# A fused two-layer block: which expert pairs of the first mixture return their rows by way of DRAM

## The chip, the core and the metric

The kernel runs on one core of a Trainium2 chip. The metric is device time in microseconds for one execution of the whole program, from inputs in DRAM to the output in DRAM; lower is better. Engines are named as in the profile: PE (TensorE) does matmuls, DVE (VectorE), ACT (ScalarE) and POOL (GpSimd) do elementwise work, SP and POOL issue DMAs. The core has 16 DMA engines that all queues share.

## The reference

Two transformer-like blocks follow each other. Each has a mixer (attention beside a recurrence), a residual addition and a mixture of experts; the second block ends in a norm that gives the output. All is in float32 with 512 tokens of width 1024. What the change touches is the first mixture: 32 experts in four groups, each token goes to the best group and there to its two best experts.

```python
def hier_moe(x2d, w_grp, b_grp, w_exp, b_exp, w_gate, w_up, w_down):
    ...
    combine = jnp.sum(jax.nn.one_hot(global_idx, N_EXPERTS, dtype=jnp.float32) * weights[..., None], axis=1)
    y = jnp.zeros_like(x2d)
    for e in range(N_EXPERTS):
        h = jax.nn.silu(x2d @ w_gate[e]) * (x2d @ w_up[e])
        y = y + combine[:, e:e + 1] * (h @ w_down[e])
    return y
...
        y = hier_moe(xn, ...)
        h = h + y.reshape(B, S, D)
```

Each expert has gate and up weights of 1024 x 256 and down weights of 256 x 1024. `combine` has two nonzero entries in a row, so a kernel need compute each expert for its own tokens alone.

## The kernel before

**Units.** The first mixture, `moe1`, works in 16 units of two experts each. An expert has 64 slots for tokens in a round, so a unit has 128 rows: expert 2u in rows 0 to 63, expert 2u+1 in rows 64 to 127. A loop behind the first round (`For_i` in `moe_rounds`, L1589) runs further rounds for experts with more than 64 tokens; here its count is zero, but every engine still loads the count (L1588), branches past the body and meets the others at a barrier, which also waits for all DMAs in flight.

**A unit's steps.** POOL gathers the unit's token rows from DRAM (`gather`, L1596, into `xg`). PE transposes them (`gathered`, L1609), multiplies by gate and up weights (L1711, `mm`), ACT and DVE make the hidden row (L1714, L1715), PE transposes it (`turned`, L1765), and in the next turn of the loop PE multiplies it by the down weights (`product`, L1655, `ua`). In the trace a float32 matmul shows as two records.

**Two ways back.** What a unit yields has to be added to the right rows of `h`, the residual stream, which stays in SBUF as four tiles of 128 tokens.

- One-hot: `down` scales the product and splits it into a high and a low half (ACT L1785, DVE L1786, tiles `oh`), and `scatter` (L1793) lets PE multiply a one-hot matrix `SC` (made by DVE, L1790) by both halves. It does so for two units at once, one half of the columns (`d`) at a time: four matmuls (L1806, L1807) for each tile of `h`, 16 for a half, summed in one PSUM bank, then one DVE add into `h` (L1800). Two banks, `ch` and `pq`, alternate.
- By DRAM: `by_dram` scales the product (ACT L1664, tile `ot`) and POOL scatters the rows to a DRAM buffer `yd` (L1665). Once the last such unit has been written, eight indirect DMAs (L1730), two for each tile of `h`, gather every token's rows from `yd` and accumulate them into `h` in SBUF. An entry of the row table out of bounds is left out.

`FROM[1]` and `BYDRAM[1]` (L28, L29) say in experts which go by DRAM: `far` (L1681) is units 4 to 13. Units 0 to 3 go by one-hot products in pairs, in the turns 3 to 6. Unit 14 and unit 15 are handled last: the down product of unit 14 is made at the start of turn 15 (`y14`), that of unit 15 behind the loop (`end`), and their one-hot products form the final pair.

**Weights.** SP loads the experts' weights, 1 MB a DMA and 96 in all (`ring_load`, L1540), into a ring of tiles `ew` in the order in which PE uses them: gate and up of a unit, then the down weights of the unit before; for unit 15 the down weights of unit 14 come first. Up to eight are in flight.

**Order.** The tile scheduler places instructions on the engines from the program's order and its own priorities; each engine runs its own list in order. In the turns from unit 9 on, the down product of a `by_dram` unit stands split on PE: two matmuls early, six later, with transposes between.

Of the kernel before, what the change touches and what calls it, by code (L numbers as in the profile page):

```python
# [24 lines left out]
SIGMOID = "sigmoid_and_others"  # L25
SILU = "silu_and_others"

FROM = {1: 8, 2: 0}  # L28
BYDRAM = {1: 20, 2: 14}  # L29
CAP = {1: 64, 2: 96}  # L30
ZROW = {k: BYDRAM[k] * CAP[k] for k in CAP}
# [38 lines left out]
def host_consts(inp):  # L70
    pc = {part: np.zeros((128, n), np.float32) for part, n in LAY.n.items()}

    def put(name, a):
        part, o, w = LAY.at[name]
        pc[part][:, o:o + w] = a

    def cols(v):
        v = np.asarray(v).reshape(-1, 128)
        return v.T
# [22 lines left out]
    for k, e in (1, np.arange(32)), (2, np.arange(16)):  # L102
        put("row%d" % k, one * np.where((e >= FROM[k]) & (e < FROM[k] + BYDRAM[k]), CAP[k] * (e - FROM[k]), 1e5))
    put("out1", i[:, None] + 128 * np.arange(16) - CAP[1] * FROM[1])
    put("g_f2", cols(inp["ffn_norm_2"]))
# [77 lines left out]
class Kern:  # L183
# [1459 lines left out]
    def moe1(self):  # L1643
# [6 lines left out]
        def product(hT, w, d):  # L1650

            p = self.ps("dn")
            for k in range(2):
                for a in range(2):
                    nc.tensor.matmul(p[hs(a)], hT[:, k, hs(a)], w[a][:, k * 1024 + d * 512:k * 1024 + d * 512 + 512],  # L1655
                                     start=k == 0, stop=k == 1)
            return p
# [10 lines left out]

        def down(hT, w, wt, SC, at=None):

            hl = []
            for d in range(2):
                y = at[:, d] if at is not None else yp.tile([128, 2, 512], R32, tag="o%d" % d, name="oh%d" % d, bufs=2 + d)
                hl.append([y[:, 0], y[:, 1]])
                self.rows_hl(*hl[d], product(hT, w, d), wt)
            return SC, hl

        def body(num, wts, idx, first):

            ys, prev = [], None  # L1680
            far = range(FROM[1] // 2, (FROM[1] + BYDRAM[1]) // 2) if first else ()  # L1681
            for u in range(2):
                ins = self.gather(xgs[u], mo, idx, u)
            if first:
                with tc.issue_after(ins.ins):
                    mo.ahead += [self.moe_load(mo, nc.gpsimd) for _ in range(mo.late)]
            nx = self.gathered(gp, xgs[0], False)

            def down_args(u, hT, num, wts):
                return hT, [self.moe_next(mo) for _ in range(2)], wts[:, u:u + 1], onehot(u, yp.tile([128, T], R32, name="SC", bufs=3))  # L1690

            onehot = lambda u, SC: self.onehot(SC, mo, num, u)
            for u in range(mo.U):
                xT, _ = nx
                if u + 2 < mo.U:
                    self.gather(xgs[u % 2], mo, idx, u + 2)
                last = u == mo.U - 1
                if last and first:
                    SC = self.place(mo, 2, R32)
                    y14 = down(prev[1], [self.moe_next(mo) for _ in range(2)], wts[:, u - 1:u], onehot(u - 1, SC[:, 0:T]),  # L1700
                               self.place(mo, 2, R32).rearrange("p (d i c) -> p d i c", d=2, i=2))
                elif last:
                    self.scatter(ys[12:14], 0)
                    ys.append(down(*down_args(*prev, num, wts)))
                w = [self.moe_next(mo) for _ in range(4)]
                p = self.ps("gu")
                for m in range(2):
                    d = p[:, m * 256:m * 256 + 256]
                    for k in range(KD):
                        for a in range(2):  # L1710
                            nc.tensor.matmul(d[hs(a)], xT[:, k, hs(a)], w[2 * m + a][:, k * 256:k * 256 + 256],  # L1711
                                             start=k == 0, stop=k == KD - 1)
                hh = gp.tile([128, 256], F32, name="hh", bufs=1)
                nc.scalar.activation(hh, p[:, 0:256], AF.Silu)  # L1714
                nc.vector.tensor_tensor(hh, hh, p[:, 256:512], OP.mult)  # L1715
                if last:
                    break
                nx = self.gathered(gp, xgs[(u + 1) % 2], False)

                e = (u - 3) // 2 * 2  # L1720
                if e >= 0 and (not first or e < far[0]):
                    self.scatter(ys[e:e + 2], (u + 1) % 2)
                if prev and prev[0] in far:
                    by_dram(*prev)
                elif prev:
                    ys.append(down(*down_args(*prev, num, wts)))
                if far and u == far[-1] + 1:
                    for c in range(2):
                        for n in range(NT):
                            nc.gpsimd.indirect_dma_start(  # L1730
                                out=self.h[:, n], out_offset=None, in_=self.yd,
                                in_offset=bass.IndirectOffsetOnAxis(ap=mo.row[:, n, c:c + 1], axis=0),
                                bounds_check=ZROW[1] - 1, oob_is_err=False, compute_op=OP.add)
                hT = gp.tile([128, 2, 128], F32, name="hT", bufs=1)
                turned(hh, hT)
                prev = u, hT
            if not first:
                self.scatter(ys[12:15], 1)
                self.scatter(ys[14:15], 0)
                hT = gp.tile([128, 2, 128], F32, name="hT", bufs=1)  # L1740
                turned(hh, hT)
                return first, None, *down_args(mo.U - 1, hT, num, wts)

            keep, gs = self.place(mo, 2), self.place(mo, 3)
            hT, wt = keep[:, 0:256].rearrange("p (k t) -> p k t", k=2), keep[:, 256:257]
            nc.vector.tensor_copy(wt, wts[:, mo.U - 1:mo.U])
            SC = onehot(mo.U - 1, SC[:, T:2 * T])
            turned(hh, hT)
            w = [self.moe_next(mo) for _ in range(2)]

            raw, hl = keep[:, D:2 * D], self.place(mo, 3, R32).rearrange("p (i k c) -> p i k c", i=2, k=KD)
            nc.sync.dma_start(raw, self.ap["win2"][4])
            raw = raw.rearrange("p (k c) -> p k c", k=KD)
            nc.scalar.activation(hl[:, 0], raw, AF.Copy)
            nc.gpsimd.tensor_tensor(hl[:, 1], raw, hl[:, 0], OP.subtract)
            self.early.append((hl[:, 0], hl[:, 1]))
            self.rows = gs[:, 0:D], gs[:, D:]
            for t, nm in zip(self.rows, ("fin_g", "attn_g")):
                nc.sync.dma_start(t, self.ap[nm].to_broadcast([128, D]))
            return first, y14, hT, w, wt, SC  # L1760
# [279 lines left out]
```

## Time and profile before

| | |
|---|---|
| median of three runs | 1422.45 us (1418.68 to 1423.33) |
| profiled execution | 1419.69 us, its span 1417.9 us |
| PE busy | 1289.0 us, 91% of the span |
| DVE, ACT, POOL busy | 841.6, 701.6, 410.2 us |
| HBM read, written | 270.70 MB, 22.29 MB |
| mean granted PE clock | 0.965 of full speed |
| chain that ended last | PE 68%, DVE 13%, DMA 11%, ACT 3%, issue 2% |

The span is the time from the first to the last instruction of one profiled execution; all times of day below count from its start. The first mixture runs from about 462 to 722 us. A share of DMA is the mean busy share of the 16 engines. "[1.63 <-DMA x]" behind a row says that the engine had been idle for 1.63 us and what ended it.

### The profile page before, as it was taken

To read this page: it belongs to the slowest core of one execution; us is meant where nothing else is said; L and a number is where in the kernel's file an instruction comes from. 1 tells how busy PE (TensorE), PEld (TensorE's weight loads), DVE (VectorE), ACT (ScalarE), POOL (GpSimd) and SP (SyncE) were. 2 spreads that over 40 slices of the span, in tenths; PEclk is the share of its full clock that TensorE was granted. 3 is DMA by queue.
4 is the path that set the end of the run, shared out by engine and by line. 5 is a ranking of instruction groups with operands and counts; after the bars stand their busy time and mean duration, and the time that the engine had idled before them with its cause. 6 is when DMAs were issued, how large, how long until landed. Compare 5 with 4: busy or idle time off the path is not lost.

```text
span 1417.9 us, 20482 instructions
## 1 busy us (share of the span) xinstructions
PE 1289.0 (91%) x7792; PEld 927.7 (65%) x7792; DVE 841.6 (59%) x1432; ACT 701.6 (49%) x1217; POOL 410.2 (29%) x329
## 2 busy tenths in 40 slices
PE   7999999999897999999379999999996999999993
PEld 5777766767696555554156776777894666666662
DVE  4679866566656131000075656657637799998895
ACT  6433433334634221211064555555545788888883
POOL 1000224241104101110366102011124555555445
PEclk9999999999998899999789999999997999999996
DMA  5232440000484999999832121202386999889943
GB/s 189 75 89 75 107 109 2 1 1 2 188 330 170 386 419 419 418 418 422 223 101 75 30 76 45 86 24 100 105 334 209 321 360 382 320 332 391 385 166 125
DMA packets 54452, 283.93 MB, mean 200 GB/s; under 512 B 8849, under 2 KB 9745, under 8 KB 28738
## 3 DMA queue, kind: packets, MB, share of 16 engines
q1 hardware_dynamic: 43634, 254.75, 47.9%
q0 software_dynamic: 9840, 26.39, 5.8%
q8 instruction: 66, 1.08, 0.3%
q10 hardware_dynamic: 864, 1.31, 0.3%
q14 instruction: 48, 0.39, 0.1%
HBM read 270.70 MB, written 22.29 MB: 207 GB/s over the span
## 4 chain that ended last, share of the span: by engine, by line
PE 68%; DVE 13%; DMA 11%; ACT 3%; issue 2%; POOL 1%; SPq 0%; DVEq 0%; POOLq 0%; ACTq 0%
PE mm L322 12%; PE ua L1903 4%; PE ua L1901 4%; PE ua L1902 4%; PE mm L1711 4%; DMA ew<-in_e1down_dram 3%; DMA ew<-in_e1up_dram 3%; PE ua L1655 2%; PE sb L322 2%; PE sb L1844 2%; PE sb L1843 2%; PE sb L1845 2%; PE sb L715 2%; DMA ew<-in_e1gate_dram 2%; DVE elo L1625 2%
## 5 line engine op out<-in xcount | busy, mean ns | idle before, releaser
L1625 DVE TENSOR_TENSOR elo<-ew,ehi 128x1024 fp32r<-128x1024 f32 x147 | 231.1, 1614 | 32.9 <-ACT ehi L1624 22.6
L1624 ACT ACTIVATE ehi<-ew 128x1024 fp32r<-128x1024 f32 x192 | 203.0, 1061 | 62.7 <-PE ua L1902 37.2
L322 PE MATMUL mm<-xh,whi 128*128 128x512 f32 (+1 forms) x384 | 155.9, 406 | 4.0 <-DVE hq L1143 3.7
L322 PE MATMUL mm<-xl,whi 128*128 128x512 f32 (+1 forms) x384 | 154.0, 401 | 0.5 <-DVE xl L354 0.3
L322 PE MATMUL mm<-xh,wlo 128*128 128x512 f32 (+1 forms) x384 | 152.8, 398 | 0.0
L1625 POOL TENSOR_TENSOR elo<-ew,ehi 128x1024 fp32r<-128x1024 f32 x45 | 125.9, 2799 | 64.8 <-ACT ehi L1624 63.0
L1711 PE MATMUL mm<-ew,xTh 128*64 128x256 f32 x1024 | 119.2, 386 | 6.4 <-DMA ew<-in_e1up_dram 4.7
L1903 PE MATMUL ua<-elo,xTh 128*96 128x512 f32 x256 | 102.9, 402 | 8.5 <-DVE elo L1625 8.4
L1711 PEld LDWEIGHTS mm<-ew,xTh 128*64 128x64 f32 x1024 | 73.5, 139 | 47.5 <-DMA ew<-in_e1up_dram 6.4
L1715 DVE TENSOR_TENSOR hh<-hh,mm 128x256 f32<-128x256 f32 x16 | 6.7, 421 | 163.5 <-ACT hh L1714 163.5
L1901 PE MATMUL ua<-ehi,xTh 128*96 128x512 f32 x256 | 102.3, 399 | 0.7 <-ACT xTh L1613 0.6
L1902 PE MATMUL ua<-ehi,xTl 128*96 128x512 f32 x256 | 101.8, 398 | 0.0
L296 ACT ACTIVATE whi<-w 128x1024 fp32r<-128x1024 f32 x53 | 55.9, 1057 | 91.1 <-PE mm L322 72.5
L297 DVE TENSOR_TENSOR wlo<-w,whi 128x1024 fp32r<-128x1024 f32 x52 | 63.7, 1227 | 51.7 <-ACT whi L296 51.5
L1596 POOL DMA_INDIRECT xg<-xd,idx x32 | 36.7, 1147 | 196.2 <-PE sb L1609 123.7
L322 PEld LDWEIGHTS mm<-xh,whi 128*128 128x128 f32 x384 | 73.4, 191 | 23.2 <-DVE hq L1143 5.4
L322 PEld LDWEIGHTS mm<-xl,whi 128*128 128x128 f32 x384 | 73.7, 192 | 16.7 <-issue 3.5
L322 PEld LDWEIGHTS mm<-xh,wlo 128*128 128x128 f32 x384 | 73.6, 192 | 16.0 <-issue 2.2
L1655 PE MATMUL ua<-ew,hT 128*64 128x512 f32 x240 | 66.4, 600 | 1.2 <-ACT hT L1766 1.1
L1714 ACT ACTIVATE hh<-mm 128x256 f32<-128x256 f32 x16 | 6.1, 383 | 112.8 <-PE mm L1711 112.8
L1903 PEld LDWEIGHTS ua<-elo,xTh 128*96 128x96 f32 x256 | 41.9, 164 | 30.6 <-DVE elo L1625 11.2
L1167 POOL TENSOR_TENSOR hAT<-hAT,hmt 128x512 f32<-128x512 f32 x16 | 22.1, 1381 | 118.9 <-DVE hmt L1166 118.3
(640 smaller groups left out, 3028.0 us busy)
## 6 DMA issues: line engine op xcount, KB each, us to landing
ew<-in_e1up_dram SPq DMA_DIRECT2D x32, 1024.0 KB, 17.8
ew<-in_e2up_dram SPq DMA_DIRECT2D x32, 1024.0 KB, 8.3
ew<-in_e2gate_dram SPq DMA_DIRECT2D x32, 1024.0 KB, 9.2
ew<-in_e2down_dram SPq DMA_DIRECT2D x32, 1024.0 KB, 12.5
ew<-in_e1gate_dram SPq DMA_DIRECT2D x31, 1024.0 KB, 19.5
ew<-in_e1down_dram SPq DMA_DIRECT2D x30, 1024.0 KB, 20.6
w<-in_win_dram SPq DMA_DIRECT2D x53, 512.0 KB, 3.6
ew<-in_wout_dram SPq DMA_DIRECT2D x8, 1024.0 KB, 6.9
```

The lines of the kernel that those rows point to most:

```text
L296: nc.scalar.activation(hi, s, AF.Copy)
L297: (eng or nc.vector).tensor_tensor(lo, s, hi, OP.subtract)
L322: mm = lambda w, x, start=False, stop=False: nc.tensor.matmul(p[:, s], w[:, k], x[:, k, s], start=start, stop=stop, skip_group_check=parts ...
L715: nc.tensor.matmul(po[d, 0:128], v[:, kb, d], wT[hh][:, kb * 128:(kb + 1) * 128], start=kb == 0, stop=kb == b)
L1596: return self.nc.gpsimd.indirect_dma_start(out=xg, out_offset=None, in_=mo.xd, in_offset=bass.IndirectOffsetOnAxis(ap=idx[:, u:u + 1], axi ...
L1624: self.hi = nc.scalar.activation(hi, s, AF.Copy)
L1625: self.lo = (nc.gpsimd if pool else nc.vector).tensor_tensor(lo, s, hi, OP.subtract)
L1655: nc.tensor.matmul(p[hs(a)], hT[:, k, hs(a)], w[a][:, k * 1024 + d * 512:k * 1024 + d * 512 + 512], start=k == 0, stop=k == 1)
L1711: nc.tensor.matmul(d[hs(a)], xT[:, k, hs(a)], w[2 * m + a][:, k * 256:k * 256 + 256], start=k == 0, stop=k == KD - 1)
L1901: nc.tensor.matmul(p, xh[:, kk], hi[:, s], start=kk == 0, stop=False)
L1902: nc.tensor.matmul(p, xl[:, kk], hi[:, s], start=False, stop=False)
L1903: nc.tensor.matmul(p, xh[:, kk], lo[:, s], start=False, stop=kk == KD - 1)
```

## The change

Units 2 to 11 go by DRAM in place of units 4 to 13, so the eight accumulating DMAs stand two turns earlier, behind the `yd` write of unit 11. Units 2 and 3 no longer return by one-hot products; units 12 and 13 do, as a pair, both halves at the start of the last turn, ahead of the down product of unit 14. Ten units go by DRAM either way.

```diff
-FROM = {1: 8, 2: 0}
+FROM = {1: 4, 2: 0}
 BYDRAM = {1: 20, 2: 14}
...
                 last = u == mo.U - 1
                 if last and first:
+                    self.scatter(ys[-2:], 0)
+                    self.scatter(ys[-2:], 1)
                     SC = self.place(mo, 2, R32)
                     y14 = down(prev[1], [self.moe_next(mo) for _ in range(2)], wts[:, u - 1:u], onehot(u - 1, SC[:, 0:T]),
```

The scheduler turns this into new orders at three places. Lines of the changed kernel from L1699 on are two higher than before (L1730 becomes L1732).

POOL's list of DMAs at the end of the first round, before (`xg` gathers, `yd` writes, `h` accumulations):

```order
L1596 DMA xg_4404<-xd_3856,idx 128x1024
L1665 DMA yd_2625<-ot,out 1280x1024
L1596 DMA xg_4405<-xd_3856,idx 128x1024
L1665 DMA yd_2625<-ot,out 1280x1024 x4
L1730 DMA h<-yd_2625,row 128x1024 x8
L1588 TENSOR_LOAD extra
```

And in the changed kernel:

```order
L1596 DMA xg_4404<-xd_3856,idx 128x1024
L1665 DMA yd_2625<-ot,out 1280x1024
L1596 DMA xg_4405<-xd_3856,idx 128x1024
L1665 DMA yd_2625<-ot,out 1280x1024 x2
L1732 DMA h<-yd_2625,row 128x1024 x8
L1588 TENSOR_LOAD extra
```

In both, the last `xg` row is the gather for unit 15. Before, four writes (units 10 to 13) stood between it and the accumulations, now two (units 10 and 11).

PE's list from the down product of unit 13 (weights `ew_5741`, `ew_5743`) through that of unit 14 (`ew_5791`, `ew_5793`), before; the gate product of unit 15 follows:

```order
L1655 MATMUL ua<-ew_5741,hT 64x512 x2
L1765 MATMUL sb<-pc_c,hh 128x128 x2
...
L1655 MATMUL ua<-ew_5743,hT 64x512
L1655 MATMUL ua<-ew_5791,hT 64x512 x2
L1655 MATMUL ua<-ew_5793,hT 64x512
L1655 MATMUL ua<-ew_5791,hT 64x512
L1655 MATMUL ua<-ew_5793,hT 64x512 x2
```

And in the changed kernel, from the down product of unit 13 (`ew_5717`); `oh_5637` and `oh_5721` are the first column halves of the results of units 12 and 13, `oh_5645` and `oh_5729` the second:

```order
L1655 MATMUL ua<-ew_5717,hT 64x512
L1808 MATMUL ch<-oh_5721,SC 128x512
L1808 MATMUL pq<-oh_5721,SC 128x512
...
L1655 MATMUL ua<-ew_5791,hT 64x512 x2
L1808 MATMUL ch<-oh_5637,SC 128x512
L1809 MATMUL ch<-oh_5637,SC 128x512
L1808 MATMUL ch<-oh_5721,SC 128x512
...
L1808 MATMUL pq<-oh_5729,SC 128x512
L1809 MATMUL pq<-oh_5729,SC 128x512
L1655 MATMUL ua<-ew_5793,hT 64x512
L1655 MATMUL ua<-ew_5791,hT 64x512
```

Of the 32 one-hot matmuls of units 12 and 13, 28 now stand between the down product of unit 13 and the second part of that of unit 14, which is split around 24 of them. The four others (unit 12 into the first two tiles) stand ahead of the gate product of unit 14.

DVE's list in the last two turns, before (`hh` is the hidden row, `ew_5796` the result of unit 14; in brackets the semaphores that a row waits for, `DMASW` those of POOL's DMAs):

```order
L1715 TENSOR_TENSOR hh<-hh,mm 128x256 [waits Activation_49]
L1746 COPY ew_5855<-wts 128x1 [waits DMAHW4_49,DMAHW3_49,DMASW2_49]
L1786 SCALAR_TENSOR_TENSOR ew_5796<-ua,wts,ew_5796 128x512 [waits DMAHW3_49,Activation_49]
L1786 SCALAR_TENSOR_TENSOR ew_5796<-ua,wts,ew_5796 128x512 [waits Activation_49]
L1715 TENSOR_TENSOR hh<-hh,mm 128x256 [waits Activation_49]
```

And in the changed kernel:

```order
L1788 SCALAR_TENSOR_TENSOR oh_5729<-ua,wts,oh_5729 128x512 [waits DMASW5_49,DMASW6_49,DMASW3_49,Activation_49]
L1802 TENSOR_TENSOR h<-h,ch 128x512 [waits DMASW1_49,PE_49]
L1802 TENSOR_TENSOR h<-h,pq 128x512 [waits DMASW2_49,PE_49]
L1802 TENSOR_TENSOR h<-h,ch 128x512 [waits DMASW3_49,PE_49]
L1802 TENSOR_TENSOR h<-h,pq 128x512 [waits DMASW4_49,PE_49]
...
L1748 COPY ew_5855<-wts 128x1 [waits DMAHW4_49,DMAHW3_49]
L1788 SCALAR_TENSOR_TENSOR ew_5796<-ua,wts,ew_5796 128x512 [waits DMAHW3_49,Activation_49]
L1788 SCALAR_TENSOR_TENSOR ew_5796<-ua,wts,ew_5796 128x512 [waits Activation_49]
L1717 TENSOR_TENSOR hh<-hh,mm 128x256 [waits Activation_49]
```

Eight adds into `h` now stand there; the first four wait for the last accumulating DMA into each of the four tiles. Before, no row of DVE waited for these DMAs ahead of the loop.

## Rows read from the trace of the kernel before

**Rows 1.** The page, forty equal slices: DMA share in tenths.

```profile
DMA  5232440000484999999832121202386999889943
```

**Rows 2.** Stretches: length, busy time of PE, PEld, DVE, ACT, POOL; PEclk, DMA share, GB/s.

```profile
480.00:640.00 160.00, 160.00 (x1098) 89.23 (x1095) 22.36 (x37) 36.33 (x70) 19.08 (x19) 1.00 1.02 419
640.00:665.00 25.00, 21.71 (x138) 10.74 (x137) 1.30 (x3) 5.25 (x10) 1.97 (x2) 1.00 1.01 421
665.00:686.00 21.00, 16.73 (x100) 8.00 (x96) 1.99 (x4) 3.40 (x6) 2.97 (x3) 1.00 0.95 393
...
692.00:698.00 6.00, 0.00 (x0) 0.00 (x0) 0.00 (x0) 0.00 (x0) 4.18 (x3) 0.62 0.97 163
...
706.00:710.00 4.00, 1.38 (x4) 0.53 (x6) 0.00 (x0) 0.00 (x0) 0.00 (x0) 0.50 0.24 84
```

**Rows 3.** PE in order of time, 640 to 716: start, length, line, tiles, count, wait.

```profile
648.50 3.67 PE L1711 MATMUL mm<-ew,xTh 128*64 128x256 f32 x30 [1.63 <-DMA ew<-in_e1up_dram]
...
664.61 3.67 PE L1711 MATMUL mm<-ew,xTh 128*64 128x256 f32 x30 [1.62 <-DMA ew<-in_e1up_dram]
668.04 1.90 PE L1655 MATMUL ua<-ew,hT 128*64 128x512 f32 x4
...
670.43 3.65 PE L1655 MATMUL ua<-ew,hT 128*64 128x512 f32 x12
675.12 3.94 PE L1655 MATMUL ua<-ew,hT 128*64 128x512 f32 x16 [1.05 <-ACT hT L1766]
...
680.88 3.67 PE L1711 MATMUL mm<-ew,xTh 128*64 128x256 f32 x32 [1.68 <-DMA ew<-in_e1gate_dram]
685.99 3.67 PE L1711 MATMUL mm<-ew,xTh 128*64 128x256 f32 x30 [1.43 <-DMA ew<-in_e1up_dram]
690.58 0.44 PE L1765 MATMUL sb<-pc_c,hh 128*128 128x128 f32 x2 [0.93 <-DVE hh L1715]
708.62 6.25 PE L1655 MATMUL ua<-ew,ew 128*64 128x512 f32 x16 [17.60 <-issue]
```

**Rows 4.** The chain that ended last, in order of time: start, length, what.

```profile
687.53 19.46 DMA h<-yd,row
707.00 1.62 issue
```

**Rows 5.** POOL in order of time, 640 to 716.

```profile
643.00 1.00 POOL L1665 DMA_INDIRECT yd<-ot,out  x1 [11.55 <-ACT hT L1766]
...
675.07 0.97 POOL L1665 DMA_INDIRECT yd<-ot,out  x1 [14.87 <-ACT hT L1766]
683.70 1.63 POOL L1730 DMA_INDIRECT h<-yd,row  x1 [7.65 <-DMA yd<-ot,out]
```

**Rows 6.** PE's branches at the first loop, L1589: ns min/median/max, first and last.

```profile
L1589 PEldq COMPARE_BRANCH  x3: 100/190/5383, 691.7 to 708.4; - x3
```

**Rows 7.** The same at the end of the second mixture.

```profile
L1589 PEldq COMPARE_BRANCH  x3: 82/187/3444, 1396.9 to 1410.9; - x3
```

**Rows 8.** DMA queues, 686 to 706 us: packets, MB, share of 16 engines.

```profile
q0 software_dynamic: 1148, 2.58, 79.9%
```

**Rows 9.** DMA queues, 640 to 660 us.

```profile
q1 hardware_dynamic: 1124, 8.18, 98.1%
```

**Rows 10.** DMA queues, 687 to 688 us.

```profile
q0 software_dynamic: 56, 0.12, 70.2%
q1 hardware_dynamic: 29, 0.15, 35.7%
```

**Rows 11.** PE at one set of one-hot matmuls, turn 3: first, last, what follows.

```profile
506.75 0.48 PE L1806 MATMUL ch<-oh,SC 128*128 128x512 f32 x1
...
510.43 0.40 PE L1807 MATMUL pq<-oh,SC 128*128 128x512 f32 x1
...
510.76 3.65 PE L1655 MATMUL ua<-ew,hT 128*64 128x512 f32 x16
```

**Rows 12.** DVE's adds into `h`, line L1800: ns min/median/max.

```profile
L1800 DVE TENSOR_TENSOR h<-h,ch x10: 677/687/690, 508.0 to 719.8; 128x512 f32<-128x512 f32 x10
```

## The prediction, made blind

> **What bounds the kernel now.** I read four views in this order: the page's forty slices, the table by stretch, the TensorE (PE) timeline with its waits, and the chain of waits. The slices show the DMA engines full for seven slices on end, the first mixture [rows 1]. The stretches say how full: a share of 1.02 at 419 GB/s from 480 to 640 us and 1.01 at 421 GB/s from 640 to 665, with PE busy 160.00 of 160 us in the one and 21.71 of 25 in the other [rows 2]. So two resources are nearly full at once. The PE timeline shows which leads at the end: from 648.50 on PE waits for weights, 1.63 us for the up weights of unit 13, 1.62 for those of unit 14, then 1.68 and 1.43 for gate and up of unit 15 [rows 3]. From there on weights land just as PE asks for them; a weight that lands later makes PE later by as much.
>
> Behind the last unit comes a hole: PE ends at 691.02 and starts again at 708.62, 17.60 us later [rows 3]. The chain says why: the accumulating DMAs that add the DRAM rows to `h` run until 707.00, then 1.62 us of sequencers [rows 4]. Their start is set by POOL's queue: the last `yd` write (unit 13) is issued at 675.07 and the first accumulation, which waits for its landing, at 683.70 [rows 5]. That hole is what the change goes for.
>
> **The change part by part.**
>
> *The accumulations move ahead by two units.* The last `yd` write is now that of unit 11, and POOL's order shows the eight accumulations right behind it, with the last gather already ahead of them, so no gather queues behind them. Before, the write of unit 11 left at 643.00 [rows 5]. PE has 8 us less to do in units 5 and 6 (below), but the down weights of unit 11 come at the pace of the full DMA engines, so I keep 643. With the 8.63 us from write to first accumulation [rows 5], they start at 652 instead of 683.70.
>
> *What is left of the hole.* PE must still leave the loop. Its last matmul ends at 691.02; a compare-and-branch then took 5.383 us at the longest [rows 6] and the waits behind the barrier 1.62 [rows 4]; with the register load and short branches between (about 1.0, from 691.02 to the branch at 692.0) that is 8.0 us. At the end of the second mixture, where the DMA engines are no longer full (the last two slices of [rows 1]), the same branch took 3.444 [rows 7]; then it is 6.1. So of 17.60 us only 9.6 to 11.5 can go. The Trainium skill, "Runtime: NRT & Kernel Launch", section Instruction fetch mechanics, says that a taken branch out of the fetched window waits for a DMA fetch. The two durations agree with that, and by it the lower of the two would hold here, where the DMA engines are then nearly idle; that moves the sum by 1.9 us.
>
> *What the accumulations cost where they go.* From 686 to 706 the software queue, which then carries nothing else, moved 2.58 MB and took 79.9% of sixteen engines for 20 us: **16.0 us of all DMA engines** [rows 8]. Weights took 98.1% of 20 us for 8.18 MB [rows 9], 2.4 us a MB; an accumulated MB costs 6.2. Before, nearly all of this lay behind the weight stream and cost it little. Now it lies in the middle of it. Is it paid in full there? In the one microsecond in which both queues had much to do, 687 to 688, the software queue had 70.2% and the weights 35.7%, together about one [rows 10]: what one takes the other loses. So I charge all 16.0 us. When does it strike? At 70% the accumulations last 16.0/0.70 = 23 us, from 652 to 675. Before, the up weights of unit 14 landed at 664.61 [rows 3], with 12.6 us of weight traffic still ahead of them at 652; of that 0.36 x 23 = 8.2 us is done when the accumulations end, so all 16.0 us come ahead of them: they land at **680.6**. The bounds of this term are 0 (the engines hide it) and 16.0 (a gain is out: traffic added ahead of the weights can't bring them sooner); I take 16.0, since rows 10 are the nearest case.
>
> *The Trainium skill weighed.* "DMA: Bandwidth & Descriptors", section Rules for kernel authors, advises to issue a DMA early, compute, and wait late; by it the accumulations would be free and the hole alone would count. The same page says under Issuing engines are not separate DMA queues that all DMAs end on the same sixteen engines and interleave. Rows 10 agree with the second; the first is the rival F below.
>
> *PE's work from there to its last matmul.* Before, from 664.61 to 691.02: 26.41 us, waits among them [rows 3]. The pair of units 12 and 13 now returns by one-hot products: 32 matmuls, of which four (unit 12 into the first two tiles) stand ahead of unit 14's products and lie in waits, so 28 remain. A set of 16 took from 506.75 to 510.76, 4.0 us [rows 11], so 28 take 7.0. The order splits the down product of unit 14 around them. Unsplit it took 3.94 us; split as in unit 13 its parts take 1.90 and 3.65 [rows 3], so +1.6. In return the two waits for gate and up of unit 15 go, 1.68 + 1.43 = 3.1, since PE is now later than its weights: their landings shift by the same 16.0. Sum 26.4 + 7.0 + 1.6 - 3.1 = 31.9, so PE's last matmul ends at 680.6 + 31.9 = **712.5**, not 691.0.
>
> *The added wait.* The first four DVE adds into `h` wait for the last accumulation into each tile. Behind them on DVE stand the low halves of unit 14's rows and the gating product of unit 15; PE's third one-hot group waits for the first add, since two banks alternate, and unit 15's products stand behind it. An add is 0.687 us [rows 12], less than a group of four matmuls, so the adds set nothing once the accumulations have landed. By the above that is about 677, while PE comes to the third group at about 692: no cost, unless they land late (rival L).
>
> *What is removed.* Units 2 and 3 lose two sets, 2 x 4.0 us of PE with 8 adds [rows 11, 12], in a stretch where the DMA share is 1.02 and nothing later waits for PE alone [rows 2]. It makes PE earlier until it runs into the weights some units on: worth nothing. The copies of results (two by ACT for each unit either way), the row splits on DVE, the one-hot masks and the count of `yd` writes, ten, only change places. SP's list of loads is the same. Behind the loop everything starts later or earlier as a whole.
>
> **The sum.** The final down product started at 708.62. Now it starts at 712.5 plus 6.1 to 8.0, so 718.6 to 720.5: **+10.0 to +11.9 us**. I take 9.5, a little below, since some of the 16.0 us may fill gaps that the DMA engines still had (a share of 0.95 from 665 to 686 [rows 2], so about one microsecond). The profiled execution took 1419.69 us (span 1417.9), 2.8 below the median 1422.45 of three runs; so 1429.2 on its own scale, **1432** on that of the median.
>
> **The rivals.**
>
> *F, faster: the accumulations are free.* The engines take them beside the weights, and only PE's additions count: 664.6 + 31.9 = 696.5, start at 702.6 to 704.5, so -4.1 to -6.0, about 1417. For it: 163 GB/s between 692 and 698 is less than half of what the engines move with weights [rows 2], so their time may be waiting rather than work. Against: the two shares of rows 10 make up one, not more. It decides the sign: below a charge of about 5 us (of 16.0) the kernel gets faster.
>
> *B, the weights alone set it.* PE catches up in the waits, and only the last weights count: the up weights of unit 15 land 16.0 later than 685.99, at 702.0, then 5.0 us to the last matmul as before [rows 3] and 6.1 to 8.0: 713.1 to 715.0, +4.5 to +6.4; with half of the charge PE's sum gives 704.5 + 6.1 to 8.0, +2.0 to +3.9. Together 1424 to 1428. For it: weights led PE until now. Against: 8.6 us of new PE work after unit 14's weights are more than the 3.1 us of waits there.
>
> *L, the accumulations land late.* Suppose weights take two thirds while both queues are full: then the accumulations last 48 us, to 700, and PE stands at the one-hot groups. Behind the last landing come an add (0.7), three groups (3.0), the rest of unit 14's down (3.65), gate and up of unit 15 (3.67 + 5.0) and the exit (6.1): 722, +13.5, 1436. Against: rows 10 give the software queue the larger part.
>
> *N, it does not do what it says:* the order could have kept the accumulations behind unit 14. The order shows them moved, so this has little left.
>
> **How the numbers follow.** Forecast 1432: 0.55. F 0.12 (1417). B 0.22 (1424 to 1428). L 0.08 (1436). N 0.03 (1422). A measurement tells 0.3% from no change, 4.3 us: 1418.2 to 1426.7. Faster: F, 0.12. Same: most of B and N, 0.20. Slower: the forecast, L and the rest of B, 0.68. The range 1418 to 1439 leaves out most of F and the upper part of L; its upper end is L plus the 2.6 us that a final down product at half clock costs against one at full (6.25 us, begun at a granted clock of 0.50, against 3.65 [rows 2, 3, 11]), should PE's longer waits bring that clock down elsewhere too.
>
> **What would show it.** The eight accumulations issued near 652 and landed by 680; the software queue's share near 0.7 and the weights' near 0.35 there; PE waiting for the up weights of unit 14 until about 680; the last matmul ahead of the loop near 712, and 6 to 8 us from there to the final down product. The forecast is wrong if the two shares add to clearly more than one, or if unit 14's weights land before 670.

## The result and the profile after

The changed kernel took 1434.91 us (median of four runs, 1433.09 to 1435.69) beside 1422.22 for the kernel before on the same chip: a ratio of 1.0092, 95% interval 1.0071 to 1.0112. It is slower by 13 us. Its profiled execution took 1433.09 us, span 1431.3. The forecast was 1432 with 1418 to 1439 around it: sign and size are right. Two of the steps that lead there are not, and their errors nearly cancel.

The forty slices of the changed kernel's page, to be held against [rows 1]: the DMA engines are full for as long, seven slices on end.

```profile
DMA  5222440000584999999522121212285999889943
```

Stretches of the changed kernel: length, busy time of PE, PEld, DVE, ACT, POOL, then PEclk, DMA share, GB/s.

```profile
480.00:640.00 160.00, 153.83 (x1061) 84.67 (x1058) 13.50 (x25) 35.77 (x69) 21.17 (x21) 1.00 1.02 419
665.00:686.00 21.00, 15.83 (x84) 7.29 (x81) 2.02 (x4) 2.04 (x4) 6.21 (x4) 0.92 1.04 340
696.00:704.00 8.00, 5.66 (x15) 3.88 (x16) 2.66 (x4) 0.00 (x0) 0.00 (x0) 0.53 0.50 209
```

From 480 to 640 PE now idles 6 us where it had been busy 160.00 of 160 [rows 2]: the 8 us of one-hot work taken out of units 5 and 6 turn into waits for weights. From 665 to 686 the engines are at least as full as before (1.04 against 0.95), but move 340 GB/s and not 393 [rows 2].

PE of the changed kernel in order of time: start, length, line, tiles, count, wait.

```profile
668.84 0.65 PE L1713 MATMUL mm<-ew,xTh 128*64 128x256 f32 x2 [0.75 <-DMA ew<-in_e1up_dram]
673.18 4.96 PE L1713 MATMUL mm<-ew,xTh 128*64 128x256 f32 x29 [3.70 <-DMA ew<-in_e1up_dram]
...
689.96 0.50 PE L1808 MATMUL pq<-oh,SC 128*128 128x512 f32 x1 [1.46 <-DVE h L1802]
690.29 0.40 PE L1809 MATMUL pq<-oh,SC 128*128 128x512 f32 x1
...
694.32 0.80 PE L1808 MATMUL ch<-oh,SC 128*128 128x512 f32 x1 [3.16 <-DVE h L1802]
694.91 0.63 PE L1809 MATMUL ch<-oh,SC 128*128 128x512 f32 x1
...
698.74 0.79 PE L1808 MATMUL pq<-oh,SC 128*128 128x512 f32 x1 [2.34 <-DVE h L1802]
...
715.40 0.44 PE L1767 MATMUL sb<-pc_c,hh 128*128 128x128 f32 x2 [0.93 <-DVE hh L1717]
721.87 6.42 PE L1655 MATMUL ua<-ew,ew 128*64 128x512 f32 x16 [6.03 <-DMA ew<-in_attn_g_dram]
```

The hole ahead of the final down product is 6.03 us in place of 17.60 [rows 3]. But PE stands three times at the one-hot groups of units 12 and 13, 7.0 us in all, and each time an add into `h` on DVE ends the wait. DVE in the same stretch says what the adds wait for, accumulations that land 4.4 us apart:

```profile
689.22 0.69 DVE L1802 TENSOR_TENSOR h<-h,pq 128x512 f32<-128x512 f32 x1 [2.73 <-DMA h<-yd,row]
693.58 0.69 DVE L1802 TENSOR_TENSOR h<-h,ch 128x512 f32<-128x512 f32 x1 [3.67 <-DMA h<-yd,row]
697.99 0.69 DVE L1802 TENSOR_TENSOR h<-h,pq 128x512 f32<-128x512 f32 x1 [3.73 <-DMA h<-yd,row]
```

POOL, which answers to [rows 5], starts to issue them where the prediction put them. The later four, the second for each tile of `h`, wait for an earlier one each, so the last leaves only at 679.66:

```profile
646.84 1.00 POOL L1665 DMA_INDIRECT yd<-ot,out  x1 [14.64 <-ACT hT L1768]
655.93 1.63 POOL L1732 DMA_INDIRECT h<-yd,row  x1 [8.09 <-DMA yd<-ot,out]
...
679.66 1.55 POOL L1732 DMA_INDIRECT h<-yd,row  x1 [3.16 <-DMA h<-yd,row]
```

DMA queues of the changed kernel, 660 to 692 us (packets, MB, share of 16 engines), against [rows 8 to 10]: over 32 us the weights keep 63%, the accumulations get 40%. The prediction had 36 and 70. The first column says why: the two queues moved almost the same number of packets, 1157 and 1109, where [rows 10] has 29 and 56.

```profile
q1 hardware_dynamic: 1157, 8.32, 63.4%
q0 software_dynamic: 1109, 2.48, 39.6%
```

PE's branches at the first loop, as [rows 6]: 3.6 us at the longest, not 5.4.

```profile
L1589 PEldq COMPARE_BRANCH  x3: 104/193/3647, 716.3 to 721.6; - x3
```

One thing is needed to compare executions: they differ by up to 4.7 us in when the mixture starts. So the table counts from PE's first gate product (463.97 before, 466.08 after) to its final down product. These two columns come from one execution of each kernel; the last two are the ratio to the kernel before on the same chip, from all runs. For e3 they differ most: its profiled execution is its fastest.

| kernel | first gate to final down, us | against before | ratio | 95% interval |
|---|---|---|---|---|
| before | 244.65 | | | |
| after | 255.79 | +11.1 | 1.0092 | 1.0071 to 1.0112 |
| e1 after, no accumulations | 237.59 | -7.1 | 0.9955 | 0.9941 to 0.9970 |
| e2 before, no accumulations | 232.30 | -12.4 | 0.9922 | 0.9904 to 0.9939 |
| e3 after, no one-hot pair | 246.69 | +2.0 | 1.0050 | 1.0033 to 1.0067 |
| e4 after, adds don't touch `h` | 246.39 | +1.7 | 1.0034 | 1.0023 to 1.0046 |
| e5 after, tile by tile | 247.52 | +2.9 | 1.0015 | 1.0005 to 1.0025 |
| e6 after, half the accumulations | 243.89 | -0.8 | 0.9999 | 0.9989 to 1.0009 |
| e7 before, plain gathers | 243.46 | -1.2 | 0.9986 | 0.9970 to 1.0001 |
| e8 after, pair written later | 251.90 | +7.3 | 1.0052 | 1.0035 to 1.0069 |
| e9 before, plain, half of the adds late | 245.99 | +1.3 | 1.0018 | 1.0008 to 1.0029 |
| e10 as e9, clearing first | 238.18 | -6.5 | 0.9944 | 0.9925 to 0.9962 |
| e11 after, pair held to the end | 252.70 | +8.1 | 1.0056 | 1.0035 to 1.0077 |

Two theories stood at the start. C, the prediction's own: the accumulations take 16.0 us of DMA from the weights, and PE's end follows from the weights. W: the weights lose less, and the time goes at the one-hot groups, which wait for accumulations that land late.

### The profile page after: what moved, and what is told of

Same layout as the page of the kernel before. It is cut to its first block, busy times and chain, and to the rows that moved or that the text cites. A ratio compares the mean times of both kernels' runs of the same rounds, so it can differ in the third digit from the quotient of the medians.

```text
span 1431.3 us, 20494 instructions
## 1 busy us (share of the span) xinstructions
PE 1301.1 (91%) x7792; PEld 934.2 (65%) x7792; DVE 841.4 (59%) x1432; ACT 702.1 (49%) x1217; POOL 411.6 (29%) x329
## 5 line engine op out<-in xcount | busy, mean ns | idle before, releaser
L1713 PE MATMUL mm<-ew,xTh 128*64 128x256 f32 x1024 | 123.0, 387 | 11.7 <-DMA ew<-in_e1up_dram 11.0
L1655 PE MATMUL ua<-ew,hT 128*64 128x512 f32 x240 | 69.9, 601 | 2.1 <-DMA ew<-in_e1down_dram 2.1
```

## Experiments 1 and 2: no accumulations

Both kernels lose the same lines.

```diff
-                if far and u == far[-1] + 1:
-                    for c in range(2):
-                        for n in range(NT):
-                            nc.gpsimd.indirect_dma_start(
-                                out=self.h[:, n], out_offset=None, in_=self.yd,
...
```

> The changed kernel without its eight accumulating DMAs: the rows of units 2 to 11 never reach h, everything else stands. It takes away their traffic and the DVE adds' wait for them together and leaves the one-hot work of units 12 and 13 in the last turn. If the accumulations (traffic or wait) are what made the change slower, PE's own sum holds: last matmul near 696, final down product at 702.6 to 704.5, so 1416 to 1418 us, under the kernel before. If the 28 one-hot matmuls and the split down product on PE are the cost, it stays at 1425 or more.

> The kernel before without its eight accumulating DMAs: the rows of units 4 to 13 never reach h. It measures how much of the 17.60 us hole ahead of the final down product belongs to them. If leaving the loop takes 6.1 to 8.0 us after PE's last matmul, as the prediction says, the hole shrinks by 9.6 to 11.5 and the time is 1411 to 1413 us. If only the 1.62 us of sequencers in the chain were fixed, the hole shrinks by 16 and the time is 1406.

Measured: 1414.80 and 1407.06 us, beside 1419.97 for the kernel before. PE of e1, then of e2:

```profile
699.09 0.44 PE L1760 MATMUL sb<-pc_c,hh 128*128 128x128 f32 x2 [0.93 <-DVE hh L1717]
705.30 6.62 PE L1655 MATMUL ua<-ew,ew 128*64 128x512 f32 x16 [5.78 <-DMA ew<-in_attn_g_dram]
```

```profile
693.94 0.44 PE L1758 MATMUL sb<-pc_c,hh 128*128 128x128 f32 x2 [0.93 <-DVE hh L1715]
699.95 1.98 PE L1655 MATMUL ua<-ew,ew 128*64 128x512 f32 x4 [5.57 <-issue]
```

Leaving the loop takes 5.6 to 5.8 us in both; 12.0 of the 17.60 us hole belonged to the accumulations, and 5.6 stay without them. Both times lie below the ranges expected, 1416 to 1418 and 1411 to 1413: the hole shrinks a little more than the 9.6 to 11.5 us, and the kernel before took 1419.97 us on this chip and not 1422.45. With the accumulations gone the changed order is 5 us faster than before, as rival F had it, so all of the loss and more comes from them: -7.1 to +11.1 is 18 us, where in the kernel before they cost 12.4. Between e1 and e2, neither with accumulations, the changed order itself costs 5.3 us in the table, about the +5.5 that the prediction added up for PE. Whether the 18 us come by traffic or by waiting, these two don't tell.

## Experiments 3 to 6: traffic or wait

e3 leaves out the one-hot pair; e4 keeps its PE work but lets the adds write elsewhere; e5 keeps everything and turns two loops, so that what lands first is asked for first; e6 issues half of the accumulations.

e3:

```diff
-                    self.scatter(ys[-2:], 0)
-                    self.scatter(ys[-2:], 1)
```

> The changed kernel without the one-hot products and adds of units 12 and 13, whose rows never reach h. The accumulations' traffic stays, and nothing on DVE or PE waits for them ahead of the loop's end. Theory C (contention: all 16.0 us of the accumulations are taken from the weights, and PE's end follows from the weights): last up weights land 16 us later than before, near 702, and the time is 1424 to 1428 us. Theory W (wait: the weights lose only about 9 us, as unit 14's landing at 673.2 against 664.6 says, and what made the change slower is the DVE adds' wait for late accumulations): last up weights at 695 to 698, last matmul at 700 to 703, 6 us to leave the loop, but the last accumulation lands near 698, so 1419 to 1423 us.

e4:

```diff
-                    self.scatter(ys[-2:], 0)
-                    self.scatter(ys[-2:], 1)
+                    self.scatter(ys[-2:], 0, away=True)
+                    self.scatter(ys[-2:], 1, away=True)
...
-            self.nc.vector.tensor_tensor(hs, hs, p, OP.add)
+            self.nc.vector.tensor_tensor(p if away else hs, self.mo.io if away else hs, p, OP.add)
```

> The changed kernel with the eight adds of units 12 and 13 writing back into their PSUM bank (a constant row plus the bank) in place of h, so their rows never reach h. PE's one-hot work and the accumulations' traffic stay; only the adds' wait for the accumulations goes. Theory C: PE then waits for the weights of unit 15 in place of the adds and ends where it did: 1433 to 1435 us. Theory W: the three stalls of 1.46, 3.16 and 2.34 us and the half clock between 694 and 703 go (about 10 us), and PE meets the last up weights at 698 at the latest: 1424 to 1428 us.

e5:

```diff
-                    self.scatter(ys[-2:], 0)
-                    self.scatter(ys[-2:], 1)
+                    for n in range(NT):
+                        for d in range(2):
+                            self.scatter(ys[-2:], d, [n])
...
-                    for c in range(2):
-                        for n in range(NT):
+                    for n in range(NT):
+                        for c in range(2):
```

> The changed kernel with two loops turned: the accumulating DMAs go tile by tile of h (both entries of a tile in a row), and the one-hot groups of units 12 and 13 too (both column halves of a tile in a row). Traffic, PE work and result are the same; the adds now ask for the tiles in the order in which they land, so PE should meet no late accumulation before the last tile. Theory W (the wait for late accumulations made 9 of the loss): as the run whose adds don't touch h, 3 to 5 us above the kernel before, 1423 to 1427 us. Theory C (contention alone): as the changed kernel, 1432 to 1435 us.

e6:

```diff
-                    for c in range(2):
+                    for c in range(1):
                         for n in range(NT):
                             nc.gpsimd.indirect_dma_start(
```

> The changed kernel with four of its eight accumulating DMAs, the first entry of each token; the other entry never reaches h. Half the traffic, and the last landing some 18 us earlier, so no wait at the one-hot groups. If traffic is paid in proportion (the run without accumulations stood 5 us under the kernel before, the run without the wait 3 to 5 over it), it lies in the middle: 1418 to 1421 us, no change against before. If all 16.0 us of the accumulations counted, half of them would give 8 us over PE's own sum: 1424 to 1427.

Measured: 1425.67 and 1423.09 (beside 1419.97), 1423.48 and 1420.94 (beside 1422.02). e3 doesn't decide: its median lies in C's range, its profiled execution (1421.73) in W's. e4 and e5 are where W put them (e4 a shade under), 8 to 9 us under the changed kernel by the table and 8 to 11 by the ratios, with all of the traffic still there. That C can't explain. e6 is where the share of the traffic put it, 1418 to 1421.

PE of e4, then the stretch of it that answers to the one at a clock of 0.53 in the changed kernel (696 to 704 there):

```profile
702.81 3.67 PE L1713 MATMUL mm<-ew,xTh 128*64 128x256 f32 x30 [1.36 <-DMA ew<-in_e1up_dram]
707.41 0.44 PE L1767 MATMUL sb<-pc_c,hh 128*128 128x128 f32 x2 [0.93 <-DVE hh L1717]
713.42 6.14 PE L1655 MATMUL ua<-ew,ew 128*64 128x512 f32 x16 [5.58 <-issue]
```

```profile
697.00:705.00 8.00, 6.63 (x55) 4.35 (x55) 1.50 (x2) 0.69 (x2) 0.00 (x0) 1.00 0.47 194
```

Without the wait PE meets the up weights of unit 15 and waits 1.36 us for them. They land 235.8 us from the first gate product, against 222.0 before: the weights do lose 13.8 us by the end, nearly the 16.0 charged. The accumulations themselves took less than 16.0 here: from 655.9 to 699 in the changed kernel 2.59 MB and 30.7% of 43.1 us, which is 13.2 us of all engines. (Two `yd` writes left the stretch; one of them took 7.8% of the 8.5 us from 675, so some 1.3 us for both. What makes up the difference to 13.8 was not traced.) e3, with 8 us less on PE, starts its final down product at the same place:

```profile
696.90 8.96 PE L1711 MATMUL mm<-ew,xTh 128*64 128x256 f32 x62 [3.41 <-DMA ew<-in_e1gate_dram]
713.09 5.91 PE L1655 MATMUL ua<-ew,ew 128*64 128x512 f32 x16 [5.86 <-issue]
```

It stands 246.69 us behind the first gate product, against 246.39 in e4, and by the medians e3 is not shorter either. So the pair's work lay in waits for weights and cost nothing there.

DVE of e5 (first row), then its PE:

```profile
702.99 0.69 DVE L1803 TENSOR_TENSOR h<-h,ch 128x512 f32<-128x512 f32 x1 [11.25 <-DMA h<-yd,row]
```

```profile
702.75 3.67 PE L1714 MATMUL mm<-ew,xTh 128*64 128x256 f32 x30 [2.73 <-DMA ew<-in_e1up_dram]
707.35 0.44 PE L1768 MATMUL sb<-pc_c,hh 128*128 128x128 f32 x2 [0.93 <-DVE hh L1718]
```

The wait is still there, 11.25 us on DVE, but it stands at the last tile, where no PE group needs the bank behind it. Same traffic, same result, 8.3 us less by the table. e5 also moves the traffic: its last accumulation leaves POOL at 693.37 and not at 679.66, since the two of a tile now follow each other. But the up weights of unit 15 land no earlier for it (237.0 us from the first gate product, 235.8 in e4), so that isn't where its gain comes from. The wait was 8 to 9 of the 11 us (e4, e5); what the weights lose is 2 to 3, net of what the shorter hole gives.

PE of e6:

```profile
673.46 5.12 PE L1713 MATMUL mm<-ew,xTh 128*64 128x256 f32 x29 [3.70 <-DMA ew<-in_e1up_dram]
...
696.46 7.07 PE L1713 MATMUL mm<-ew,xTh 128*64 128x256 f32 x60
...
710.42 5.62 PE L1655 MATMUL ua<-ew,ew 128*64 128x512 f32 x16 [5.53 <-DMA ew<-in_attn_g_dram]
```

It lies at the kernel before: with half of the traffic and no wait the change is worth nothing either way. Here PE meets unit 15's weights without a wait, and the terms of the prediction's sum can be read off one by one: +6.3 at unit 14, +5.0 of PE, -12.1 of the hole, together -0.8.

## Experiments 8 and 11: where the pair's work stands

In both, the two calls at the start of the turn are gone. e8 writes them behind the products of unit 15:

```diff
                 if last:
+                    if first:
+                        self.scatter(ys[-2:], 0)
+                        self.scatter(ys[-2:], 1)
                     break
```

> The changed kernel with all 32 one-hot matmuls of units 12 and 13 placed behind the up product of unit 15, where every accumulation has landed; the result is the same. No wait for accumulations is left, as in the run whose adds don't touch h, but the one-hot work now stands behind the last weights. If that work was free only because PE waited for weights, it costs its 7.5 us here: 1429 to 1432 us. If it is hidden wherever it stands, 1423 to 1425.

e11 holds them there by an order:

```diff
-                            nc.tensor.matmul(d[hs(a)], xT[:, k, hs(a)], w[2 * m + a][:, k * 256:k * 256 + 256],
+                            mmi = nc.tensor.matmul(d[hs(a)], xT[:, k, hs(a)], w[2 * m + a][:, k * 256:k * 256 + 256],
...
                 if last:
+                    if first:
+                        with tc.issue_after(mmi.ins):
+                            self.scatter(ys[-2:], 0)
+                            self.scatter(ys[-2:], 1)
                     break
```

> The changed kernel with all 32 one-hot matmuls of units 12 and 13 held behind the last matmul of unit 15's up product (in the run with the two calls merely written there, the scheduler still put most of them ahead of it); the result is the same. Every accumulation has landed by then, so no wait for them is left. What is asked is whether the one-hot work was free in the run whose adds don't touch h, because it lay in PE's waits for weights. If so, here it stands behind the last weights and costs its 32 x 0.235 = 7.5 us over that run (3 over the kernel before): 1430 to 1434 us. If PE was never waiting there and the order of its work doesn't matter, 1423 to 1426.

Measured: 1429.07 (beside 1422.02) and 1430.37 (beside 1420.30). e8 hit its number for another reason than it gave: the calls stand later in the program, but the scheduler still put the groups ahead of most of unit 15's products, with the second half of unit 14's down product between them. It is a case of half the wait, two stalls of 3.7 us together and not three of 7.0:

```profile
691.93 0.50 PE L1809 MATMUL pq<-oh,SC 128*128 128x512 f32 x1 [1.44 <-DVE h L1803]
...
700.70 0.50 PE L1809 MATMUL pq<-oh,SC 128*128 128x512 f32 x1 [2.30 <-DVE h L1803]
...
719.94 5.17 PE L1655 MATMUL ua<-ew,ew 128*64 128x512 f32 x16 [5.91 <-DMA ew<-in_attn_g_dram]
```

e11 holds them by an order. No stall for an accumulation is left, and the 32 matmuls fill the time between the up product of unit 15 and PE's last transpose:

```profile
703.26 3.67 PE L1711 MATMUL mm<-ew,xTh 128*64 128x256 f32 x30 [0.56 <-DMA ew<-in_e1up_dram]
...
714.77 0.38 PE L1769 MATMUL sb<-pc_c,hh 128*128 128x128 f32 x2
720.47 5.33 PE L1655 MATMUL ua<-ew,ew 128*64 128x512 f32 x12 [5.32 <-issue]
```

Against e4 that is 6.3 us later in the table, a little less than the 7.5 expected. The pair is free ahead of the last weights and paid for behind them.

## Experiments 7, 9 and 10: a cheaper way back

The accumulations themselves are what is dear, in either place. These three take the kernel before and gather the rows into cleared tiles, without adding; DVE adds them.

e7 takes the accumulating DMAs out and has behind the weights of unit 15, in the last turn:

```diff
+            back = [self.place(mo, 1) for _ in range(NT)]
+            for b in back:
+                nc.vector.memset(b, 0.0)
+            for n in range(NT):
+                for c in range(2):
+                    nc.gpsimd.indirect_dma_start(
+                        out=back[n][:, c * D:c * D + D], out_offset=None, in_=self.yd,
+                        in_offset=bass.IndirectOffsetOnAxis(ap=mo.row[:, n, c:c + 1], axis=0),
+                        bounds_check=ZROW[1] - 1, oob_is_err=False)
+            for n in range(NT):
+                for c in range(2):
+                    nc.vector.tensor_tensor(self.h[:, n], self.h[:, n], back[n][:, c * D:c * D + D], OP.add)
```

> The kernel before, with the eight accumulating DMAs replaced by eight plain gathers into four cleared tiles at the same place and eight DVE adds into h behind them; the result is the same. If an accumulated MB is dear because the DMA adds (6.2 us a MB here against 2.7 in the plain gathers at the end of the second mixture), the gathers take 7 us of all engines in place of 16 and the hole is bound by POOL's issues: eight of 1.3 to 1.6 us from 683.7, the last landing 5 later near 701, add and barrier behind it, final down product near 704 and not 708.6: 1414 to 1417 us. If the row-wise access is what is dear, nothing changes: 1420 to 1422.

e9, against e7; `returned` is the two adds of a tile, and its second place is in `end`, behind the loop:

```diff
-            back = [self.place(mo, 1) for _ in range(NT)]
+            back = [self.place(mo, 0 if n > 1 else 1) for n in range(NT)]
...
+            self.back, ins = back, None
+            for n in range(2):
+                with tc.issue_after(ins.ins) if ins else ExitStack():
+                    ins = self.returned(n)
...
+                for n in range(2, NT):
+                    self.returned(n)
```

> As the plain gathers before, but only the adds of the first two tiles of h stand ahead of the loop; those of the other two stand behind it, so that the barrier waits for the gathers alone and not for all eight adds on DVE. In the run before this one the last gather landed 702.0 and the last add ended at 709.9, with two adds of 3.0 and 3.4 us beside POOL's work, and the final down product began at 710.4. If the adds were what held it, the final down product begins about 1.6 to 2.5 us behind the last landing, near 704 to 705, and the four adds of 1.22 us behind the barrier lie beside it: 1413 to 1416 us. If leaving the loop is bound elsewhere, as the run with eight adds: 1418 to 1421.

e10, against e9:

```diff
-                nc.vector.tensor_tensor(hh, hh, p[:, 256:512], OP.mult)
+                ins = nc.vector.tensor_tensor(hh, hh, p[:, 256:512], OP.mult)
...
-                nc.vector.memset(b, 0.0)
+                clear = nc.vector.memset(b, 0.0)
...
-                with tc.issue_after(ins.ins) if ins else ExitStack():
+                with tc.issue_after(ins.ins), tc.issue_after(clear.ins):
```

> As the run before it, with the four clearing writes on DVE held ahead of unit 15's hidden row and the adds of the first two tiles behind it. In the run before, the first add stood ahead of two of them, so POOL issued the last four gathers from 697.1 on and the last landed at 708.8. With the clearing done near 691 all gathers should be issued by 697 and landed by 702, as in the first run with plain gathers; nothing but landings then holds the barrier: final down product near 704 (711.6 in the run before), the last add into h some 5 us earlier than there, 1414 to 1417 us. If two adds beside POOL's work still take 3.0 to 3.4 us each behind the barrier, the gain at the final down product is given back and the time is 1418 to 1420.

Measured: 1419.32 (beside 1422.02), 1423.80 (beside 1421.96), 1415.60 (beside 1422.17). e7 missed its 1414 to 1417: the gathers did land by 702, but the adds took their place. Its POOL, its DVE, and the line of the adds (ns min/median/max):

```profile
697.28 2.34 POOL L1761 TENSOR_TENSOR ew<-ew,ew 128x1024 fp32r<-128x1024 f32 x1 [0.17 <-ACTq L1589]
699.80 3.09 POOL L402 TENSOR_TENSOR ew<-ew 128x1024 f32<-128x1024 f32 x1 [0.18 <-SPq L1589]
```

```profile
697.72 12.18 DVE L1755 TENSOR_TENSOR h<-h,ew 128x1024 f32<-128x1024 f32 x7 [2.76 <-DMA ew<-yd,row]
```

```profile
L1755 DVE TENSOR_TENSOR h<-h,ew x8: 1210/1224/3354, 693.7 to 708.7; 128x1024 f32<-128x1024 f32 x8
```

Seven adds end at 709.9, and the loop's barrier waits for them. Two of the seven, from 697.72 and 700.62, took 2.98 and 3.35 us beside POOL's two rows; the other five took 1.2 each. e9 missed its 1413 to 1416 too: the scheduler put the first add ahead of two of the clearing writes, so POOL issued the last four gathers only from 697.11:

```profile
697.11 4.08 POOL L1749 DMA_INDIRECT ew<-yd,row  x1 [6.66 <-DVE hh L1715]
```

With that order mended, e10 does what was wanted. Its software queue from 686 to 706, against [rows 8], and its PE and DVE:

```profile
q0 software_dynamic: 1194, 2.57, 38.4%
```

```profile
706.89 5.14 PE L1655 MATMUL ua<-ew,ew 128*64 128x512 f32 x16 [9.79 <-issue]
```

```profile
706.73 6.91 DVE L1795 TENSOR_TENSOR h<-h,ew 128x1024 f32<-128x1024 f32 x4 [2.35 <-issue]
```

The hole is 9.79 us, and the four late adds lie beside the final down product. At 0.9944 it beats both kernels. It differs from the kernel before in more than the engines' time: POOL issues a gather in about 1.0 us and not in 1.55 to 1.63, none waits for another of its tile, and half of the adds stand behind the loop. How its gain divides among these was not tested.

## Why the prediction was right, and where it was wrong

**Where the accumulations start: right.** Counted from the first gate product, 189.9 us against the 188.0 forecast.

**What is left of the hole: right, a little high.** 6.03 us against 6.1 to 8.0; in e1 to e4 5.6 to 5.9. The branch took 3.3 us with idle DMA engines (e2, a share of 0.02 to 0.09) and 3.6 in the changed kernel, where two other loads ran beside its second half, not 5.4 as before with full ones. The Trainium skill, "Runtime: NRT & Kernel Launch", section Instruction fetch mechanics, has such a branch wait for a DMA; these rows agree.

**The charge to the weights: nearly right in size, wrong in time.** The step that failed first is the share. It was taken from rows 10, one microsecond in which the weights were running out (29 packets against 56). With both queues full, packets went one for one (1157 and 1109), and the accumulations got 0.40. The rows of before had this in them: at 98.1% of 20 us for 1124 packets [rows 9] and 79.9% for 1148 [rows 8], one for one would give the accumulations an estimated 0.44. So unit 14's up weights came 6.5 us late (207.1 from the first gate product against 200.6), not 16.0; the last ones 13.8 (e4), beside 13.2 us that the accumulations took of the engines in the changed kernel.

**The added wait: wrong.** "The adds set nothing once the accumulations have landed", near 677, rests on that same share. At 0.40 the 13.2 us that they took last 33. Nothing of them moved before 660; 2.48 of 2.59 MB had moved by 692, and the last add that waited for one began at 697.99; PE stood 7.0 us at the groups. The forecast also had all eight issued without a break; POOL stood 11.8 us in waits for the first four. How much of the late landing is due to these waits was not tested. PE's stalls were followed by a granted clock of 0.53 from 696 to 704, about the lower of the two levels (1.2 of 2.4 GHz): a one-hot matmul took 0.63 us and not 0.40. In e4, without the stalls, the clock was 1.00 there. This is rival L, near enough in its split (two thirds for the weights), and it gave 722 for the final down product: it is at 721.87, in an execution whose mixture started 2.1 us later. It had 0.08.

**PE's work: right by itself, and beside the point.** From unit 14's up weights to the last matmul 31.9 us were forecast; without accumulations it took 29.8 (e1, 669.76 to 699.53), with half of them 31.4 (e6), in the changed kernel 42.7. But in e3 and e4, with and without the pair, PE ended at the same place. Rival B, the weights alone, describes the kernel as soon as the wait is gone: its +4.5 became +1.7 to +2.9, from 13.8 in place of 16.0 and a faster exit.

**The sum.** Forecast: +16.0 at unit 14, +5.5 of PE, -9.6 to -11.5 of the hole, 10.0 to 11.9. Measured: +6.5, +16.2, -11.6, which is +11.1. The 9.5 us that the charge missed came back as 7.0 of stalls and, by an estimate from the rows, 3 of half clock (fifteen matmuls at some 0.2 more). Both errors go back to the share: while the accumulations last, either the weights are late or the accumulations are, so what it takes from one term it gives to the other. That the two came out nearly equal is luck all the same. With accumulations and adds in another order (e5) the same traffic costs 8.3 us less, and 1432 would have been some 7 us too high.

**The signs named.** The first accumulation was issued near 652 as said (655.9, or 653.8 with the later start taken off). Landed by 680, a share near 0.7 and a wait for unit 14's weights until 680 did not come true: 697.99, 0.40 and 673.18. The last matmul near 712 (715.84) and the exit of 6 to 8 us did, the former for another reason. The two shares add to 1.03.

**Removed sets: right.** Worth nothing; PE waits for the weights it has caught up with.

**Rival F** was right on what it would be worth: 4.1 to 6.0 were forecast for free accumulations, e1 has 5.2 in the median. The point where the sign turns, a charge of 5 of the 16.0 us, is borne out in part: half of them, a charge of 6.3 at unit 14 (e6), gives no change.

## What to carry to other kernels

Where DMA engines are full, a transfer that is brought forward from behind the stream into it is still paid for, and it lands late itself, since it shares the engines: before making anything wait for it, work out its landing from a stretch in which both queues are full (here packets went one for one), not from the end of the stream. If something must wait, ask for the pieces in the order in which they land, and put the wait where no other engine's buffer hangs on it (e5 gave back 8 of 11 us so). And here cheaper traffic beat better placed traffic: the same rows, gathered without adding, took half the time of the engines.

## What the runs showed of the hardware

- An accumulating indirect DMA cost twice the plain one: 2.58 MB at 79.9% of 20 us, 16.0 us [rows 8], against 2.57 MB at 38.4%, 7.7 us (e10), with the same rows and the same table. In the middle of the weight stream the accumulating ones took 13.2 us (the changed kernel, 655.9 to 699).
- A DVE add of two SBUF tiles took 1.22 us, but 2.98 and 3.35 where POOL's elementwise work lay beside (e7). The Trainium skill, "SBUF — State Buffer", section SBUF: two separate sides, says that a DVE operation with two SBUF inputs and a GpSimd operation that reads SBUF lock each other out of a shared port pair; these rows agree.
- The share of a queue was not fixed: the weights had 0.36 in their last microsecond [rows 10], and 0.63 with both queues full, when packets went one for one (1157 and 1109 in 32 us). An accumulating DMA then landed 12.8 to 18.5 us after its issue, against 6.3 to 9.2 in the kernel before.
